# Streaming encoder trunk, one core: the MLP up projection with four PSUM banks, sums of squared outputs on VectorE, a new memory order at the turn to the MLP, and the last product gated from PSUM

## The chip, the cores and the metric

The kernel runs on one core of one Trainium2 chip. The metric is the device time of one execution in microseconds (us); smaller is better. Before the change the median of 3 runs is 2645.79 us (2639.45 to 2650.24). The profile is of one more execution, of 2640.47 us.

## The reference, cut to what matters

One layer: a modulated RMSNorm, an input projection shared by an mLSTM and a short convolution, an output projection, and then the squared-ReLU MLP that the change is about. 2048 prompt tokens and 128 sample tokens go through the same weights; sample tokens have their own modulation values (`mod`), one set for each group of 16 tokens.

```python
x = x + gt1 * (mix @ w_out)
h2 = _rms(x) * g2 * (1 + sc2) + sh2
x = x + gt2 * (jnp.square(jax.nn.relu(h2 @ w_up)) @ w_down)
...
y_prompt = _rms(xp) * g_final
```

D_MODEL is 1024, the MLP is 4096 wide, everything is float32.

## The kernel before, in words

**Attention.** The first stage (lines 200 to 830) does everything up to the first residual, in six blocks of tokens. It writes the residual x to DRAM (`x1s`) and a scale for each token (`x1r`). The up projection of the MLP begins when it has ended.

**Fast matrix product.** Each product of the MLP is made on 2x2 blocks with seven products in place of eight (a Winograd form), numbered 1 to 7, in the order of `ORDER` (L876): 1, 6, 5, 7, 2, 4, 3. A float32 operand is split in two float32r parts: ScalarE makes `hi` (L872, L1009, L1077), VectorE makes `lo = x - hi` (L873, L1010, L1078; GpSimd for two of the seven token operands, L1010), and TensorE does hi*hi, hi*lo and lo*hi (`mm12`, L934, every matmul is on L938).

**Up projection.** The tokens go in three passes p = 0, 1, 2 of two halves of 364, 364 and 360 tokens (`HALVES`). `stage_load` (L955) fetches the tokens of a pass, `stage_mod` (L969) multiplies by the scale (L972, on GpSimd) and applies the modulation (L979 to L982), `stage_split` (L984) makes the sums of blocks (L992, L993, L998, L1003) and the seven operands `h1` to `h7`. In each pass 16 units j = 0 to 15 follow (`up_unit`, L1013). A unit does the seven products, 12 matmuls each, so 84 matmuls. Its weights are fetched one unit ahead (`fetch_w`, L883) and split one unit ahead (`prep_w`, L896); in pass 0 the sums of weight blocks are also made (L902, four a unit) and written out (L903), and passes 1 and 2 read them back. In passes 1 and 2 sixteen calls of `sums_down` (L916) make the sums of the down weights: six in pass 1, ten in the first units of pass 2.

A unit has three PSUM banks, each with two buffers. Products 1 and 2 accumulate in bank 0, products 6, 7 and 4 in bank 1, products 5 and 3 in bank 2 (`where`, L1017). Between them VectorE reads the partial sums: product 7 adds onto 6 in the bank after L1028 has read it, product 4 adds onto 7 after L1030 has read it. Then ScalarE does ReLU and Square (L1039, L1040), GpSimd makes the sums of the squared outputs that the down projection needs (L1041 to L1043, three instructions), and SP's queue stores the tile (L1044).

**Down projection.** `open_down` (L1048) frees the memory of the up stage. Three passes of four groups g and seven products q follow; each of these 84 steps fetches a token operand (L1066) and a weight block (L1068), splits them (`d_prep`), does 2 x 24 matmuls (`d_mul`, L1082) and adds the result to an accumulator (L1095). In the last group, `combine` (L1107) joins accumulators and `close` (L1127) gates the result into y and adds its squares for the last RMSNorm (ScalarE L1146, GpSimd L1147). `final` (L1149) sums the squares over partitions on TensorE (L1153), scales y (L1159) and stores it (L1160).

**What sets the order.** TensorE runs in the order of the program. On the other engines the framework orders the instructions at build time by their place in the program and by when its own model of time has their inputs ready; each engine and SP's queue then run strictly in that order. Memory pools are laid out one behind the other; the MLP's pools lie over those of attention, and a tile waits for the tiles that it lies over to be dead (`open_up`, L940).

Of the kernel before, what the change touches and what calls it, by code (L numbers as in the profile page):

```python
# [9 lines left out]
F32 = mybir.dt.float32  # L10
# [34 lines left out]
def tile_hybrid(ctx: ExitStack, tc: tile.TileContext, xT, cst, early, rows_in, vgb, wada,  # L45
# [786 lines left out]
    def stats_last():  # L832
# [3 lines left out]
        ps = ps_.tile([128, 512], F32, name="st", tag="st")[:, :n]  # L836
# [39 lines left out]
    ORDER = (1, 6, 5, 7, 2, 4, 3)  # L876
# [63 lines left out]
    def open_up():  # L940
        pA.close()
        up = B["up"] = ctx.enter_context(ExitStack())

        def p(name, **kw):
            return up.enter_context(tc.tile_pool(name=name, reuse_waits="tile", **kw))

        B["ct"] = p("bct", bufs=2)
        B["nb"] = p("bnb", bufs=1)
        B["h"] = p("bh", bufs=1)
        B["stg"] = p("bstg", bufs=1)  # L950
        B["wr"] = p("bwr", bufs=1)
        B["wl"] = p("bwl", bufs=1)
        B["ps"] = p("bps", bufs=1, space=PSUM)

# [14 lines left out]
    def stage_mod(p, c, kh):  # L969
        t0, n = HALVES[2 * p + c]  # L970
        x = B["st"][:, c + 2 * kh, :, :n]
        pool.tensor_tensor(x, x, B["r"][:, c, :n].unsqueeze(1).to_broadcast([128, 4, n]), MUL)  # L972
        for k in range(4):
            kk = 4 * kh + k
            for a, b, smp in segments(t0, n):
                z = x[:, k, a:b]
                if smp:
                    z3 = z.rearrange("p (b s) -> p b s", b=NB)
                    dve.tensor_tensor(z3, z3, modT[:, 4, kk, 1:9].unsqueeze(2).to_broadcast([128, NB, TS]), MUL)  # L979
                    dve.tensor_tensor(z3, z3, modT[:, 3, kk, 1:9].unsqueeze(2).to_broadcast([128, NB, TS]), ADD)  # L980
                else:
                    act.activation(z, z, AF.Identity, scale=modT[:, 4, kk, 0:1], bias=modT[:, 3, kk, 0:1])  # L982

    def stage_split(p, q):  # L984
        n = HALVES[2 * p][1]
        st = B["st"]
        b11, b12, b21, b22, t2 = (st[:, j, :, :n] for j in range(5))
        i = ORDER[q]
        if i == 1:
            src = b11  # L990
        elif i == 6:
            dve.tensor_tensor(b12, b12, b11, SUB)  # L992
            dve.tensor_tensor(t2, b22, b12, SUB)  # L993
            src = t2
        elif i == 5:
            src = b12
        elif i == 7:
            dve.tensor_tensor(b11, t2, b11, SUB)  # L998
            src = b11
        elif i == 2:  # L1000
            src = b21
        elif i == 4:
            dve.tensor_tensor(b21, b21, t2, SUB)  # L1003
            src = b21
        else:
            src = b22
        hi = B["h"].tile([128, 4, HN], F32R, name=f"h{i}hi", tag=f"h{i}hi")[:, :, :n]
        lo = B["h"].tile([128, 4, HN], F32R, name=f"h{i}lo", tag=f"h{i}lo")[:, :, :n]
        act.activation(hi, src, AF.Copy)  # L1009
        (pool if q in (2, 5) else dve).tensor_tensor(lo, src, hi.bitcast(F32), SUB)  # L1010
        B["hc", i] = (hi, lo)

    def up_unit(p, j, between):  # L1013
        n = HALVES[2 * p][1]
        ct = B["ct"].tile([128, 7, n], F32, name="ct", tag="ct")
        banks = [B["ps"].tile([128, 512], F32, name=f"bk{z}", tag=f"bk{z}", bufs=2)[:, :n] for z in range(3)]
        where = {1: 0, 2: 0, 6: 1, 7: 1, 4: 1, 5: 2, 3: 2}  # L1017
        begun = {1, 6, 5}
        c11, c12, c21, c22 = (ct[:, z] for z in (0, 1, 2, 3))
        for q, i in enumerate(ORDER):  # L1020
            w, h = W[p, j, i], B["hc", i]
            bk = banks[where[i]]
            mm12(bk, [(w[0][:, k], w[1][:, k]) for k in range(4)], [(h[0][:, k], h[1][:, k]) for k in range(4)],
                 i in begun)
            if i == 1:
                act.activation(c21, bk, AF.Copy)
            elif i == 6:
                dve.tensor_tensor(c12, c21, bk, ADD)  # L1028
            elif i == 7:
                dve.tensor_tensor(c22, c21, bk, ADD)  # L1030
                dve.tensor_tensor(c22, c22, banks[2], ADD)
            elif i == 2:
                act.activation(c11, bk, AF.Relu)
            elif i == 4:
                dve.tensor_tensor(c21, c21, bk, ADD)
            elif i == 3:
                dve.tensor_tensor(c12, c12, bk, ADD)
# [44 lines left out]
    def d_mul(p, g, q, cd):  # L1082
# [24 lines left out]
    def combine(p, cd, i):  # L1107
# [12 lines left out]
        elif i == 4:  # L1120
            dve.tensor_tensor(a[4], a[7], a[4], SUB)  # L1121
            close(p, cd, 0, 1, a[4])
# [4 lines left out]
    def close(p, cd, ch, mh, z):  # L1127
        t0, n = HALVES[2 * p + ch]
        for c2 in range(2):
            k = 4 * mh + 2 * cd + c2  # L1130
            y = B["yt"][:, ch, k]
            for b0, b1, smp in segments(t0, n):
                d, yy = z[:, c2, b0:b1], y[:, b0:b1]
                if smp:
                    d3 = d.rearrange("p (b s) -> p b s", b=NB)
                    dve.tensor_tensor(d3, d3, modT[:, 5, k, 1:9].unsqueeze(2).to_broadcast([128, NB, TS]), MUL)
                    dve.tensor_tensor(yy, yy, d, ADD)
                else:
                    dve.scalar_tensor_tensor(yy, d, modT[:, 5, k, 0:1], yy, MUL, ADD)  # L1139
            if (p, ch) not in B["ssk"]:  # L1140
                B["ssk"].add((p, ch))
                B["ss", ch] = B["nb"].tile([128, HN], F32, name=f"ss{ch}", tag=f"ss{ch}")[:, :n]
                act.activation(B["ss", ch], y, AF.Square)
            else:
                sq = B["nb"].tile([128, HN], F32, name="bsq", tag="bsq", bufs=2)[:, :n]
                act.activation(sq, y, AF.Square)  # L1146
                pool.tensor_tensor(B["ss", ch], B["ss", ch], sq, ADD)  # L1147

    def final(p, ch):  # L1149
# [3 lines left out]
        pe.matmul(ps, ones, B["ss", ch], start=True, stop=True)  # L1153
# [220 lines left out]
```

## Time and profile before

| what | value |
|---|---|
| median of 3 runs | 2645.79 us |
| the profiled execution | 2640.47 us, span 2638.7 us |
| TensorE (PE) busy | 2424.5 us, 92% |
| VectorE (DVE) busy | 1930.8 us, 73% |
| ScalarE (ACT) busy | 1271.6 us, 48% |
| GpSimd (POOL) busy | 723.5 us, 27% |
| granted TensorE clock, mean | 0.969 |
| DMA | 540.75 MB, 205 GB/s |

The span is from the first to the last instruction. PE is the matrix engine, PEld its weight loads, SPq the queue of the engine that issues DMAs. A row of a group of instructions names line, engine, operation and tiles as out<-in; behind "|" come busy time and mean length, and the idle time of the engine just before. A row of a stretch gives its bounds and length, the busy time of PE, PEld, DVE, ACT and POOL with the number of their instructions, the mean granted TensorE clock as a share of full speed, the busy share of the DMA engines and what they moved. A row of a tile gives the shortest, median and longest instruction in ns.

### The profile page before, as it was taken

How to read it: one execution, taken by the hardware profiler on the slowest of the kernel's cores; microseconds unless marked ns; L12 is line 12 of the kernel's file. 1: busy time of each engine (PE TensorE's matmuls, PEld its weight loads, DVE VectorE, ACT ScalarE, POOL GpSimd, SP SyncE). 2: the span in 40 equal slices, each digit the busy share in tenths (PEclk: the TensorE clock that was granted, in tenths of full speed). 3: DMA queues.
4: the chain of work that ended last, by engine and by line, in shares of the span. 5: the costliest groups of instructions: out<-in, count | busy, mean ns of one | idle time of the engine just before them, and what ended most of it. 6: DMA issues, size and time to landing. Idle time of an engine off the chain costs nothing. (4 is left out here: it accounts for less than half of the span.)

```text
span 2638.7 us, 38838 instructions
## 1 busy us (share of the span) xinstructions
PE 2424.5 (92%) x14849; PEld 2349.5 (89%) x14849; DVE 1930.8 (73%) x2595; ACT 1271.6 (48%) x1989; POOL 723.5 (27%) x570
## 2 busy tenths in 40 slices
PE   7999899999999999579989989888899989999996
PEld 5899888999999999578889989888899989999996
DVE  5578876776767757787777677766647796788779
ACT  3455554544544535544455455434554455445443
POOL 1244433343423413442233243322300040002003
PEclk9999999999999999799999999999999999999998
DMA  7645466354353443456667875878776658657762
GB/s 298 207 136 195 137 215 212 109 175 127 90 191 107 135 134 111 148 198 223 233 209 245 311 247 202 285 255 298 261 267 228 227 176 313 228 192 272 263 234 101
DMA packets 208918, 540.75 MB, mean 205 GB/s; under 512 B 31632, under 2 KB 88464, under 8 KB 190300
## 3 DMA queue, kind: packets, MB, share of 16 engines
q1 hardware_dynamic: 203564, 514.33, 57.7%
q0 software_dynamic: 5168, 23.94, 2.7%
q8 instruction: 117, 1.92, 0.3%
q14 instruction: 69, 0.57, 0.1%
HBM read 420.83 MB, written 117.37 MB: 204 GB/s over the span
## 5 line engine op out<-in xcount | busy, mean ns | idle before, releaser
L872 ACT ACTIVATE whi<-wraw 128x512 fp32r<-128x512 f32 (+1 forms) x504 | 382.2, 771 | 593.4 <-PE dn L938 275.5
L873 DVE TENSOR_TENSOR wlo<-wraw,whi 128x512 fp32r<-128x512 f32 (+1 forms) x504 | 535.6, 1078 | 99.0 <-ACT whi L872 97.1
L938 PE MATMUL dn<-ulo,whi 128*128 128x364 f32 (+1 forms) x1344 | 445.0, 331 | 21.5 <-DVE ulo L1078 21.5
L938 PE MATMUL dn<-uhi,whi 128*128 128x364 f32 (+1 forms) x1344 | 446.3, 332 | 7.5 <-ACT uhi L1077 7.5
L938 PE MATMUL dn<-uhi,wlo 128*128 128x364 f32 (+1 forms) x1344 | 442.1, 329 | 0.0
L121 PE MATMUL mm<-hhi,whi 128*128 128x384 f32 (+1 forms) x1152 | 388.9, 338 | 1.1 <-DVE kT L462 0.7
L122 PE MATMUL mm<-hlo,whi 128*128 128x384 f32 (+1 forms) x1152 | 381.4, 331 | 0.0
L123 PE MATMUL mm<-hhi,wlo 128*128 128x384 f32 (+1 forms) x1152 | 380.1, 330 | 0.1
L80 ACT ACTIVATE whi<-wraw 128x1024 fp32r<-128x1024 f32 (+1 forms) x216 | 227.0, 1054 | 235.9 <-PE mm L122 142.5
L81 DVE TENSOR_TENSOR wlo<-wraw,whi 128x1024 fp32r<-128x1024 f32 (+1 forms) x184 | 243.9, 1328 | 93.3 <-ACT whi L80 92.9
L938 PEld LDWEIGHTS dn<-ulo,whi 128*128 128x128 f32 x1344 | 255.3, 190 | 24.5 <-DVE ulo L1078 24.3
L938 PEld LDWEIGHTS dn<-uhi,whi 128*128 128x128 f32 x1344 | 254.7, 189 | 8.2 <-ACT uhi L1077 7.8
L938 PEld LDWEIGHTS dn<-uhi,wlo 128*128 128x128 f32 x1344 | 255.6, 190 | 0.0
L1147 POOL TENSOR_TENSOR ss<-ss,bsq 128x364 f32<-128x364 f32 (+1 forms) x42 | 72.5, 1727 | 639.2 <-ACT bsq L1146 637.7
L121 PEld LDWEIGHTS mm<-hhi,whi 128*128 128x128 f32 x1152 | 219.4, 190 | 10.0 <-issue 6.8
L122 PEld LDWEIGHTS mm<-hlo,whi 128*128 128x128 f32 x1152 | 219.3, 190 | 0.7
L123 PEld LDWEIGHTS mm<-hhi,wlo 128*128 128x128 f32 x1152 | 219.1, 190 | 0.3 <-DVE wlo L81 0.3
L1041 POOL TENSOR_TENSOR ct<-ct 128x364 f32<-128x364 f32 (+1 forms) x48 | 49.3, 1027 | 496.6 <-ACT ct L1040 484.4
L1095 DVE TENSOR_TENSOR a<-a,dn 128x728 f32<-128x728 f32 (+1 forms) x126 | 114.4, 908 | 91.1 <-PE dn L938 87.6
L1078 DVE TENSOR_TENSOR ulo<-ur,uhi 128x1456 fp32r<-128x1456 f32 (+1 forms) x84 | 144.3, 1717 | 25.4 <-ACT uhi L1077 21.4
L122 PE MATMUL mm<-mlo,whi 128*128 128x384 f32 (+1 forms) x384 | 126.6, 330 | 3.9 <-POOL mlo L627 3.9
L123 PE MATMUL mm<-mhi,wlo 128*128 128x384 f32 (+1 forms) x384 | 127.1, 331 | 1.4 <-DVE wlo L81 1.3
(330 smaller groups left out, 5575.7 us busy)
## 6 DMA issues: line engine op xcount, KB each, us to landing
wraw<-wsd SPq DMA_DIRECT2D x48, 1024.0 KB, 4.9
wraw<-wup SPq DMA_DIRECT2D x160, 256.0 KB, 5.6
us<-ct SPq DMA_DIRECT2D x32, 1274.0 KB, 5.3
ur<-us SPq DMA_DIRECT2D x56, 728.0 KB, 5.6
wraw<-wbcx SPq DMA_DIRECT2D x72, 512.0 KB, 3.8
wraw<-wdown SPq DMA_DIRECT2D x36, 1024.0 KB, 5.0
wraw<-wsu SPq DMA_DIRECT2D x128, 256.0 KB, 5.9
wraw<-wout SPq DMA_DIRECT2D x48, 512.0 KB, 3.6
```

Source lines behind the costliest of these rows:

```text
L80: act.activation(hi[:, :n], raw[:, :n], AF.Copy)
L81: ins = eng.tensor_tensor(lo[:, :n], raw[:, :n], hi[:, :n].bitcast(F32), SUB).ins
L121: pe.matmul(out, lh[0], rh[0], start=first, stop=False)
L122: pe.matmul(out, lh[0], rh[1], start=False, stop=False)
L123: pe.matmul(out, lh[1], rh[0], start=False, stop=last)
L872: act.activation(hi, src, AF.Copy)
L873: dve.tensor_tensor(lo, src, hi.bitcast(F32), SUB)
L938: pe.matmul(out, lh, rh, start=first and z == 0, stop=z == len(seq) - 1, skip_group_check=not first)
L1041: pool.tensor_tensor(c12, c12, c11, SUB)
L1078: dve.tensor_tensor(lo, raw, hi.bitcast(F32), SUB)
L1095: dve.tensor_tensor(a, a, ps, ADD)
L1147: pool.tensor_tensor(B["ss", ch], B["ss", ch], sq, ADD)
```

## The change

- **Up banks.** Four banks of two buffers (two sets of four) in place of three. `ORDER` becomes 1, 6, 5, 7, 2, 3, 4. Products 1 and 2 share bank 0, 6 and 3 bank 1, 7 and 4 bank 3, 5 has bank 2. Product 3 starts its bank anew; only 2 and 4 add onto what the bank holds.
- **Sums of squared outputs.** Four VectorE instructions in place of three of GpSimd, made in the next unit after its second product, with the store behind them. One difference changes sign, and so does the use of product 4 in the down projection.
- **Tokens of a pass.** Three of the four scalings of `stage_mod` move from GpSimd to VectorE; the sample modulation is one instruction over four blocks in place of four; the sums of blocks become `stage_sum`, called at listed places; pass 1's tokens are loaded at unit 8 in place of 11; GpSimd makes the `lo` of products 3 and 4 in place of 5 and 4.
- **Memory.** The raw weight tiles come first in memory, the operands of products 1 and 6 last, and the other operands in a listed order.
- **Down projection, last group.** Before product 4, accumulator 7 is added to accumulator 4 and the sum is gated into y; product 4's own last group is then gated straight from PSUM. In the last pass, the last two squares are summed by TensorE; `final` of half 1 is called between the two halves of the last product.

```diff
-        ps = ps_.tile([128, 512], F32, name="st", tag="st")[:, :n]
+        ps = ps_.tile([128, 512], F32, name="st", tag="bk0", bufs=2)[:, :n]
...
-    ORDER = (1, 6, 5, 7, 2, 4, 3)
+    ORDER = (1, 6, 5, 7, 2, 3, 4)
...
+        B["wr"] = p("bwr", bufs=1)
         B["ct"] = p("bct", bufs=2)
         B["nb"] = p("bnb", bufs=1)
-        B["h"] = p("bh", bufs=1)
+        late, soon = p("bh", bufs=1), None
         B["stg"] = p("bstg", bufs=1)
-        B["wr"] = p("bwr", bufs=1)
         B["wl"] = p("bwl", bufs=1)
+        soon = p("bh16", bufs=1)
+        B["h"] = {i: soon if i in (1, 6) else late for i in ORDER}
...
-        pool.tensor_tensor(x, x, B["r"][:, c, :n].unsqueeze(1).to_broadcast([128, 4, n]), MUL)
+        eng = pool if (c, kh) == (0, 1) else dve
+        eng.tensor_tensor(x, x, B["r"][:, c, :n].unsqueeze(1).to_broadcast([128, 4, n]), MUL)
...
+    def stage_sum(p, z):
+        n = HALVES[2 * p][1]
+        b11, b12, b21, b22, t2 = (B["st"][:, j, :, :n] for j in range(5))
+        o, x, y = ((b12, b12, b11), (t2, b22, b12), (b11, t2, b11), (b21, b21, t2))[z]
+        dve.tensor_tensor(o, x, y, SUB)
...
-        (pool if q in (2, 5) else dve).tensor_tensor(lo, src, hi.bitcast(F32), SUB)
+        (pool if q > 4 else dve).tensor_tensor(lo, src, hi.bitcast(F32), SUB)
...
-        banks = [B["ps"].tile([128, 512], F32, name=f"bk{z}", tag=f"bk{z}", bufs=2)[:, :n] for z in range(3)]
-        where = {1: 0, 2: 0, 6: 1, 7: 1, 4: 1, 5: 2, 3: 2}
-        begun = {1, 6, 5}
+        banks = [B["ps"].tile([128, 512], F32, name=f"bk{z}", tag=f"bk{z}", bufs=2)[:, :n] for z in range(4)]
...
-            bk = banks[where[i]]
+            bk = banks[{1: 0, 2: 0, 6: 1, 3: 1, 5: 2, 7: 3, 4: 3}[i]]
             mm12(bk, [(w[0][:, k], w[1][:, k]) for k in range(4)], [(h[0][:, k], h[1][:, k]) for k in range(4)],
-                 i in begun)
+                 i not in (2, 4))
...
+            else:
+                o, x = {6: (c21, c21), 5: (c12, c21), 7: (c22, c12), 3: (c12, c12), 4: (c21, c21)}[i]
+                dve.tensor_tensor(o, x, bk, ADD)
             between(q)
         act.activation(ct[:, 1:4], ct[:, 1:4], AF.Relu)
         act.activation(ct[:, 0:4], ct[:, 0:4], AF.Square)
-        pool.tensor_tensor(c12, c12, c11, SUB)
-        pool.tensor_tensor(ct[:, 4], c22, c12, SUB)
-        pool.tensor_tensor(ct[:, 5:7], ct[:, 4:5].to_broadcast([128, 2, n]), ct[:, 0:3:2], SUB)
-        nc.sync.dma_start(us[p][j // 4][:, j % 4], ct.rearrange("p a b -> p (a b)"))
+
+        def sums():
+            dve.tensor_tensor(c12, c12, c11, SUB)
+            dve.tensor_tensor(ct[:, 4], c22, c12, SUB)
+            dve.tensor_tensor(ct[:, 5], ct[:, 4], c11, SUB)
+            dve.tensor_tensor(ct[:, 6], c21, ct[:, 4], SUB)
+            nc.sync.dma_start(us[p][j // 4][:, j % 4], ct.rearrange("p a b -> p (a b)"))
+
+        B["sums"] = sums
...
+            if mid and c2 == 0:
+                mid()
+        if g == 3 and i == 4:
+            with tc.high_priority():
+                close(p, cd, 0, 1, ps, True)
+            return
...
-        elif i == 4:
-            dve.tensor_tensor(a[4], a[7], a[4], SUB)
-            close(p, cd, 0, 1, a[4])
...
+            if late and cd and p == NP - 1:
+                B["more"].append(sq)
+            else:
                 pool.tensor_tensor(B["ss", ch], B["ss", ch], sq, ADD)
...
+        parts = [B["ss", ch], *(B["more"] if p == NP - 1 and ch == 0 else [])]
+        for z, sq in enumerate(parts):
+            pe.matmul(ps, ones, sq, start=z == 0, stop=z == len(parts) - 1)
+        v, y0, t, r = (nb.tile([128, HN], F32, name=f"f{z}", tag=f"f{z}", bufs=2)[:, :n] for z in "vytr")
...
+        hl = ("2hi", "2lo", "7hi", "3hi", "3lo", "4hi", "4lo", "7lo", "5lo", "5hi")
+        for z in hl:
+            late.tile([128, 4, HN], F32R, name=f"h{z}", tag=f"h{z}")
...
+            mods = ((10, 3), (11, 3), (12, 3), (13, 3)) if p == 0 else ((13, 1), (13, 4), (14, 1), (14, 3))
+            for at_, (c, kh) in zip(mods, parts):
+                z[at_] = [(stage_mod, (p + 1, c, kh))]
+            for at_, k in zip(((14, 0), (14, 2)) if p == 0 else ((14, 5), (14, 6)), (0, 1)):
+                z.setdefault(at_, []).append((stage_sum, (p + 1, k)))
+            for q in range(7):
+                z[15, q] = [(stage_sum, (p + 1, {3: 2, 6: 3}[q]))] if q in (3, 6) else []
+                z[15, q].append((stage_split, (p + 1, q)))
...
-            if j == 11 and p + 1 < NP:
+            if p + 1 < NP and j == (8, 11)[p]:
...
+                if q == 1 and before:
+                    before()
...
+            if g == 3 and ORDER[q] == 4:
+                for cd in range(2):
+                    a = B["a", p, 4, cd]
+                    dve.tensor_tensor(a, a, B["a", p, 7, cd], ADD)
+                    gate(p, cd, 0, 1, a)
...
-            d_mul(p, g, q, 1)
+            d_mul(p, g, q, 1, (lambda: final(p, 1)) if end else None)
...
         final(NP - 1, 0)
-        final(NP - 1, 1)
```

`gate` is the first half of the old `close`; it no longer writes the product of a sample segment in place, but into a tile `gs`.

## Rows read from the trace of the kernel before

**Rows 1.** Stretches: bounds, length, busy time by engine, clock, DMA share, GB/s.

```profile
1084.00:1108.00 24.00, 0.00 (x1) 0.00 (x0) 18.51 (x33) 10.66 (x23) 6.09 (x5) 0.55 0.53 169
1108.00:1134.00 26.00, 18.83 (x87) 17.58 (x88) 25.65 (x24) 14.00 (x18) 7.86 (x2) 0.82 0.22 70
1134.00:1367.00 233.00, 204.99 (x1177) 200.80 (x1176) 178.81 (x227) 112.74 (x170) 73.91 (x46) 0.96 0.64 224
1367.00:1409.00 42.00, 32.89 (x169) 32.29 (x168) 37.44 (x35) 23.75 (x29) 16.68 (x8) 0.84 0.50 166
1409.00:1625.00 216.00, 201.81 (x1179) 199.68 (x1178) 148.66 (x190) 113.37 (x170) 71.95 (x46) 0.98 0.79 273
...
1666.00:1833.00 167.00, 148.14 (x843) 143.37 (x841) 107.49 (x150) 70.57 (x104) 41.96 (x30) 0.96 0.82 287
1833.00:1908.00 75.00, 70.30 (x420) 68.49 (x419) 49.36 (x65) 40.74 (x59) 21.79 (x15) 1.00 0.74 258
1908.00:2613.00 705.00, 676.79 (x4017) 673.31 (x4018) 542.71 (x522) 338.45 (x346) 67.05 (x38) 0.98 0.67 233
2613.00:2638.70 25.70, 6.41 (x29) 4.47 (x27) 21.44 (x32) 5.93 (x12) 9.02 (x8) 0.69 0.29 115
...
1597.00:1625.00 28.00, 28.00 (x170) 28.00 (x169) 18.20 (x24) 14.93 (x22) 8.10 (x6) 1.00 0.65 223
```

**Rows 2.** What TensorE waited for, 1080 to 1910 us (total, times, longest).

```profile
PE bk L938 <- DVE ct L1030: 46.7, 20, 7.9
PE bk L938 <- DVE ct L1028: 33.1, 11, 5.0
PE bk L938 <- ACT h1hi L1009: 24.3, 1, 24.3
```

**Rows 3.** VectorE, then GpSimd, in order of time, 1139 to 1152 us (start, length).

```profile
1140.15 10.12 DVE L902 TENSOR_TENSOR wraw<-wraw 128x512 f32<-128x512 f32 x4
...
1151.40 0.52 DVE L1030 TENSOR_TENSOR ct<-ct,bk 128x364 f32<-128x364 f32 x1
...
1139.66 2.09 POOL L1043 TENSOR_TENSOR ct<-ct 128x728 f32<-128x728 f32 x1
1141.70 7.42 POOL L972 TENSOR_TENSOR stg<-stg,rst 128x1456 f32<-128x1456 f32 x2
```

**Rows 4.** Instructions of single tiles in the up stage (ns, min/median/max).

```profile
L873 DVE TENSOR_TENSOR wlo<-wraw,whi x332: 674/691/3800, 1123.7 to 1899.4; 128x512 fp32r<-128x512 f32 x164, 128x1024 fp32r<-128x1024 f32 x2
...
L1030 DVE TENSOR_TENSOR ct<-ct,bk x48: 515/520/533, 1129.1 to 1901.3; 128x364 f32<-128x364 f32 x32, 128x360 f32<-128x360 f32 x16
...
L1010 DVE TENSOR_TENSOR h7lo<-stg,h7hi x3: 1658/1660/1675, 1120.1 to 1645.4; 128x1456 fp32r<-128x1456 f32 x2, 128x1440 fp32r<-128x1440 f32 x1
```

**Rows 5.** Costliest VectorE groups, 1108 to 1910 us (busy, mean ns).

```profile
L873 DVE TENSOR_TENSOR wlo<-wraw,whi 128x512 fp32r<-128x512 f32 (+1 forms) x332 | 326.1, 1003 | 48.0 <-ACT whi L872 47.9
L902 DVE TENSOR_TENSOR wraw<-wraw 128x512 f32<-128x512 f32 x60 | 53.8, 907 | 7.4 <-DMA wraw<-wup 6.7
```

**Rows 6.** ScalarE in order of time at the turn to the MLP.

```profile
1106.30 0.63 ACT L872 ACTIVATE whi<-wraw 128x512 fp32r<-128x512 f32 x1 [6.88 <-DMA wraw<-wup]
1106.84 1.40 ACT L1009 ACTIVATE h1hi<-stg 128x1456 fp32r<-128x1456 f32 x1
```

**Rows 7.** The stretch with the fullest DMA engines, columns as in rows 1.

```profile
1500.00:1520.00 20.00, 17.85 (x108) 17.55 (x107) 11.08 (x18) 10.90 (x17) 4.47 (x4) 1.00 0.99 357
```

**Rows 8.** The chain that ended last, from the up to the down projection (start, length).

```profile
1903.88 9.26 DMA ur<-us
...
1916.39 13.67 PE dn L938 x72
```

**Rows 9.** The same chain behind the last matmuls.

```profile
2623.93 5.37 DVE y L1159 x8
...
2632.09 3.02 DVE y L1159 x6
```

**Rows 10.** ScalarE in order of time, a unit that began at 1245.0 us.

```profile
1247.56 1.40 ACT L1040 ACTIVATE ct<-ct 128x1456 f32<-128x1456 f32 x1
```

More of the change, by code (lines that the diff above doesn't have):

```diff
@@ new lines, in stage_mod @@
+        eng.tensor_tensor(x, x, B["r"][:, c, :n].unsqueeze(1).to_broadcast([128, 4, n]), MUL)
+        for a, b, smp in segments(t0, n):
+            if smp:
+                for v, op in ((4, MUL), (3, ADD)):
+                    z4 = x[:, :, a:b].rearrange("p k (b s) -> p k b s", b=NB)
+                    m4 = modT[:, v, 4 * kh:4 * kh + 4, 1:9].unsqueeze(3).to_broadcast([128, 4, NB, TS])
+                    dve.tensor_tensor(z4, z4, m4, op)
+            else:
+                for k in range(4):
+                    kk = 4 * kh + k
+                    act.activation(x[:, k, a:b], x[:, k, a:b], AF.Identity, scale=modT[:, 4, kk, 0:1],
+                                   bias=modT[:, 3, kk, 0:1])
@@ L1125, in combine, with gate @@
             close(p, cd, 1, 0, a[3])
-    def close(p, cd, ch, mh, z):
+    def gate(p, cd, ch, mh, z):
         t0, n = HALVES[2 * p + ch]
@@ L1134, in close @@
                 if smp:
-                    d3 = d.rearrange("p (b s) -> p b s", b=NB)
-                    dve.tensor_tensor(d3, d3, modT[:, 5, k, 1:9].unsqueeze(2).to_broadcast([128, NB, TS]), MUL)
-                    dve.tensor_tensor(yy, yy, d, ADD)
+                    t = B["nb"].tile([128, 128], F32, name="gs", tag="gs")
+                    t3 = t.rearrange("p (b s) -> p b s", b=NB)
+                    dve.tensor_tensor(t3, d.rearrange("p (b s) -> p b s", b=NB),
+                                      modT[:, 5, k, 1:9].unsqueeze(2).to_broadcast([128, NB, TS]), MUL)
+                    dve.tensor_tensor(yy, yy, t, ADD)
                 else:
                     dve.scalar_tensor_tensor(yy, d, modT[:, 5, k, 0:1], yy, MUL, ADD)
+    def close(p, cd, ch, mh, z, late=False):
+        n = HALVES[2 * p + ch][1]
+        gate(p, cd, ch, mh, z)
+        for c2 in range(2):
+            y = B["yt"][:, ch, 4 * mh + 2 * cd + c2]
             if (p, ch) not in B["ssk"]:
@@ L1143, in close @@
                 act.activation(B["ss", ch], y, AF.Square)
[L1144 to L1146 removed]
+                continue
+            sq = B["nb"].tile([128, HN], F32, name="bsq", tag="bsq", bufs=2)[:, :n]
+            act.activation(sq, y, AF.Square)
+            if late and cd and p == NP - 1:
+                B["more"].append(sq)
+            else:
                 pool.tensor_tensor(B["ss", ch], B["ss", ch], sq, ADD)
@@ L1183, in phase_b, with between @@
                 sums += 1
-            def between(q, p=p, j=j, nxt=nxt):
+            def between(q, p=p, j=j, nxt=nxt, before=B["sums"]):
                 if nxt:
                     prep_w(*nxt, q)
-                if p + 1 < NP:
-                    if j in (13, 14) and q in (1, 4):
-                        stage_mod(p + 1, *((0, 0), (1, 0), (1, 1), (0, 1))[2 * (j - 13) + (q == 4)])
-                    if j == 15:
-                        stage_split(p + 1, q)
+                if q == 1 and before:
+                    before()
+                for fn, args in plan.get(p, {}).get((j, q), ()):
+                    fn(*args)
                 if z == 0 and q == 2:
@@ L1196, in phase_b @@
             up_unit(p, j, between)
+        B["sums"]()
         assert sums == 16
@@ L1199, in phase_b @@
         B["ssk"] = set()
+        B["more"] = []
         ds = [(p, g, q) for p in range(NP) for g in range(4) for q in range(7)]
@@ L1204, in phase_b @@
         for z, (p, g, q) in enumerate(ds):
+            end = z + 1 == len(ds)
             if z + 2 < len(ds):
@@ L1208, in phase_b @@
                 y_load(p)
+            if g == 3 and ORDER[q] == 4:
[3 more added lines that the diff above has]
+                    gate(p, cd, 0, 1, a)
             d_mul(p, g, q, 0)
-            if z + 1 < len(ds):
+            if not end:
                 d_prep(*ds[z + 1])
```

63 lines of the change are left out of this document (17 added, 46 removed).

## The prediction

> **What bounds the kernel now.** I read the stretches first, then TensorE's waits, then single instructions of the engines that it waits for. Two full units of the up projection at an unbroken pace take 28.0 us [rows 1], so a unit costs 14.0 us when nothing holds TensorE, and 360/364 of that, 13.85 us, in pass 2. Against this the stretches show what is lost. The turn from attention and the first unit take 24 + 26 us for 14 us of work: 36 lost. Units 1 to 14 of pass 0 take 233 us for 196: 37 lost. The last unit of pass 0 with the first of pass 1 takes 42 us for 28, and the other change of pass, of 41 us, looks the same: 27 lost in both. Units 1 to 14 of pass 1 lose 216 - 196 = 20, the first ten after that in pass 2 167 - 138.5 = 28.5, the last five 75 - 69 = 6. That is 154 us in a stage where TensorE has nothing to wait for but other engines; the down projection with 705 us for some 4000 matmuls is close to its pace [rows 1]. The waits say for whom: 46.7 us for L1030 and 33.1 us for L1028, the reads of a bank that the next product adds onto, and 24.3 us for the first operand h1hi [rows 2]. The rest of the loss is the slow clock behind such a wait: 0.82 in the first unit, 0.84 at the change of pass, 0.96 in pass 0, of 2.4 GHz [rows 1].
>
> Why is L1030 late? It takes 0.52 us each time, but it stands in VectorE's queue behind L902 and L873, and these are held up: four L902 took 10.12 us in a row while GpSimd ran L1043 and two L972 of 7.42 us together [rows 3]. Alone, L873 takes 0.69 us, at most 3.80 [rows 4]; its mean is 1.00 us, so 332 of them lost about 104 us in the stage [rows 5]. L1030, which reads one input from PSUM, never took over 0.533 us [rows 4]. So an operation of VectorE with both inputs in SBUF waits for GpSimd's, and a PSUM read waits only in the queue.
>
> **The change, part by part.**
>
> Four banks. Product 7 no longer adds onto 6, and product 4 adds onto 7 with two products between them in place of one. The wait of 33.1 us has no more cause, and L1030's successor has 4.1 us in place of 2.1 us before it is missed. The number of reads stays at five a unit, of 0.52 us. The two sets fill all eight banks; unit j+1 writes the set that unit j-1 has left. The single reading of the sum for the last block's statistics takes one buffer of bank 0 once, hidden in unit 0's lost time.
>
> Sums on VectorE. Four instructions of 364 columns from SBUF; the nearest rows are 0.52 us for the same width with one input in PSUM and 0.69 us for 512 columns [rows 4]. I take 0.55, so 2.2 us a unit. VectorE then has in a unit of pass 0: seven L873 and four L902 of 0.69, five reads of 0.52, the sums: 7.6 + 2.6 + 2.2 = 12.4 us of 14.0. In pass 1 it is 9.7, with four more of 0.69 us in units that also sum down weights. This holds if GpSimd is quiet, and what is left to GpSimd is one L972 of 3.7 us a pass and two `lo`. The sums wait for ScalarE's Square; behind them in VectorE's queue stand the reads of products 6, 5 and 7. The Square of a unit ends 4.0 us into the next one [rows 10], just when the sums come up, so they should not wait. Their store follows in SP's queue, 2 us earlier than now.
>
> Units 1 to 14 of pass 0: of the 37 us I leave 4, for the three scalings (1.66 us each, as L1010 of the same width [rows 4]) and late weights: -33, between -5 (VectorE as now) and -37. Units 1 to 14 of pass 1: -15 of 20, between -4 and -20, since weights come by DMA here. First ten units of pass 2: they move 167 us x 287 GB/s = 47.9 MB [rows 1]; at the fullest stretch, 357 GB/s with DMA engines 0.99 busy [rows 7], that takes 134 us, hardly under the 138.5 us of TensorE. Between no gain and -28.5 I take half, -14. Last five units: -3 of 6.
>
> Changes of pass: in the last unit VectorE has 9.7 us of its own, five `lo` and two sums of blocks of 1.66 us [rows 4], in all 21 us against 14, and GpSimd still runs two `lo` that hold VectorE up. Some 7 us over is then lost each time in place of 13.5: -13, between 0 and -20.
>
> Turn from attention. The last matmul of attention ends at 1084; ScalarE made h1hi only at 1106.84, right behind a split that had waited 6.88 us for a weight of unit 1 [rows 6]. In the new memory order the operands of products 1 and 6 lie over attention tiles that are dead before its last product, and the weights' raw tiles over those of attention, of which the first are read by then. So h1 can be made before TensorE is free. Product 6 still needs all four scalings, and VectorE has in the first unit five `lo` and four sums of blocks (15 us), weight splits and sums of the next unit (7.6 us) and five reads (2.6 us): 25 us for 14. I leave 3 + 10 = 13 of the 36 us: -23, between -8 and -33.
>
> Start of the down projection. The first token operand was asked for at 1903.88, landed 9.26 us later, and TensorE began at 1916.4 [rows 8]. By my count of the pools its tile will lie over an operand of product 4, which is now the last to be read, at the end of the up stage, some 3.5 us later: +3.5, between 0 and +8.
>
> Last group of the down projection. For each half of product 4 an accumulation and a difference of 0.9 us go, an addition of 0.9 us and two more gates come; VectorE's work is the same within 1 us, and it is VectorE that ends the kernel: eight L1159 took 5.37 us, and the last six of the other half 3.02 us [rows 9]. `final` of half 1 can fill waits of the chain of half 0 in place of following it, but its matmul now stands inside the last product and may hold TensorE for 1 to 2 us until GpSimd's last sum. I take -3, between +2 and -8.
>
> Sum: -33 - 15 - 14 - 3 - 13 - 23 + 3.5 - 3 = -100.5, against the profiled execution's 2640.5 us: 2540 us. That execution lies 5.3 us under the median of the runs before, so a median may lie as much above my figure.
>
> **Rivals.**
>
> VectorE becomes the bound. It is busy for 178.8 of 233 us in pass 0, 37.4 of 42 us at the change of pass and 25.7 of 26 us in the first unit [rows 1], and it is given 48 x 2.2 = 106 us of GpSimd's work. If its operations stay as long as their means now, 1.00 and 0.91 us [rows 5], and the sums stretch alike to 0.75 us, a unit of pass 0 needs 7.0 + 3.6 + 2.6 + 3.0 = 16.3 us. Then pass 0 gains 37 - 14 x 2.3 = 5 us, the six units of pass 1 with down weights lose 14 so that 6 are gained, pass 2 gains 4, the changes of pass nothing: 2640.5 - 23 - 5 - 6 - 4 - 3 + 3.5 - 3 = 2600. For it speaks the busy share; against it rows 3, where the stretch goes with GpSimd's work, which leaves. The Trainium skill (Perfetto Trace Analysis, Optimizing Scalar/DVE Operations) advises the other direction, to offload a saturated VectorE to ScalarE or even GpSimd, which would make this the likelier case and 2600 the sum. The same paragraph warns that GpSimd and VectorE share an SBUF read port, so that moving work between the two might not help, and with that the trace agrees: 10.12 us of L902 beside 7.42 us of L972 [rows 3]. Chance 0.12.
>
> The memory order does not do what it says at the turn: h1hi still stands behind a split that waits for a weight, or the raw tiles over attention's bring the weights late. The 36 us stay, and the rest goes as forecast: 2563. For it, ScalarE ran h1hi in queue order behind a DMA [rows 6]. Chance 0.08.
>
> Slower: a ring through VectorE's queue. The sums stand ahead of the reads of products 6, 5 and 7; if Square comes late, VectorE stands still, product 4 waits for its bank, TensorE frees weight buffers late, ScalarE's splits wait for these and Square behind them comes late again. Product 4 begins 12 us into a unit, so with 2 us of sums this decides from a Square later than 10 us into the unit, against 4.0 us now [rows 10]. A stall of 2.1 us in each of 48 units takes back the 100.5 us; one of 3 us gives 2540 + 144 = 2684. Chance 0.04.
>
> **How the numbers follow.** The forecast has 0.76. Its own range, with the ends of the three largest terms not all at once, is 2512 to 2578. The range 2508 to 2600 adds the unshortened turn and half of the VectorE case; left out are the slower case, the other half and some of the forecast's own edges, together under 0.2. A measurement of this kernel tells some 0.5%, 13 us, from no change: faster than 2632 by the first three cases, 0.94; the slower case splits into 0.04 beyond and little near zero, to which I add 0.02 for small mishaps in sum.
>
> **What would show it.** Right: TensorE's waits for reads of banks fall from 80 us to under 20; L873's mean falls to about 0.72 us; units of pass 0 take 14.0 us; TensorE waits under 8 us at the turn; the ten units of pass 2 show DMA engines over 0.9 busy. The forecast is wrong if VectorE is over 95% busy in pass 0 with waits for wlo in place of the reads, if h1hi is again made over 15 us after attention's last matmul, or if VectorE waits for Square in most units.

## The result, and the profile after

The changed kernel takes 2567.4 us (median of four runs, 2566.9 to 2572.1), the kernel before 2647.7 in the same comparison: ratio 0.971, 95% interval 0.968 to 0.973. Its profiled execution took 2567.2 us with a span of 2565.1, so 73.6 us of span are gone (80.3 by the medians) where 100.5 were forecast. By stretch, as in [rows 1]:

```profile
1084.00:1092.00 8.00, 0.00 (x0) 0.00 (x0) 8.00 (x8) 4.67 (x12) 3.18 (x4) 0.75 0.60 179
1092.00:1122.00 30.00, 20.22 (x84) 18.00 (x85) 28.75 (x29) 15.32 (x20) 8.98 (x3) 0.73 0.43 144
1122.00:1325.00 203.00, 198.55 (x1182) 198.19 (x1181) 166.92 (x292) 112.69 (x174) 3.60 (x1) 0.99 0.72 253
1325.00:1363.00 38.00, 30.27 (x169) 29.41 (x168) 33.61 (x40) 23.29 (x30) 11.93 (x2) 0.93 0.68 227
1363.00:1560.00 197.00, 197.00 (x1177) 196.53 (x1176) 147.28 (x254) 113.11 (x170) 4.39 (x1) 1.00 0.88 305
1560.00:1596.00 36.00, 29.71 (x169) 28.85 (x168) 32.67 (x38) 23.31 (x29) 11.27 (x2) 0.96 0.46 158
1596.00:1753.00 157.00, 144.78 (x842) 142.73 (x841) 110.24 (x197) 73.58 (x107) 0.00 (x0) 0.97 0.90 314
1753.00:1822.00 69.00, 69.00 (x423) 68.97 (x421) 42.34 (x77) 35.72 (x52) 0.00 (x0) 1.00 0.68 253
...
1840.40:2565.10 724.70, 678.43 (x4002) 673.48 (x4000) 559.10 (x557) 338.35 (x352) 60.97 (x40) 0.97 0.64 224
```

Units 2 to 14 of pass 0, units 1 to 14 of pass 1 and the last five of pass 2 now run at TensorE's pace, with at most 0.7 us over in one of them. Unit 1 of pass 0 (20.2 us for 14.0) does not, nor do these: the turn (8 + 30 us), the changes of pass (38, and 36 for the other) and the first ten units of pass 2 (157 for 138.5). The last line is the down projection from its second step to the end: 724.7 us, before 713.0. It got longer, which no term of the sum foresaw.

What TensorE waits for, 1080 to 1910 us, beside [rows 2]:

```profile
PE bk L938 <- DVE ct L1021: 22.5, 9, 4.6
PE bk L938 <- ACT ct L1016: 12.2, 7, 2.6
PE bk L938 <- ACT whi L872: 11.1, 2, 8.7
...
PE bk L938 <- DVE wlo L873: 3.3, 2, 2.5
```

The reads of banks (now all L1021) cost 22.5 us for 80, and stand in the first units and at the changes of pass alone. New is L1016, ScalarE's copy of product 1. VectorE's own largest wait and then its groups, as in [rows 5]:

```profile
DVE ct L1027 <- ACT ct L1024: 67.4, 37, 2.7
```

```profile
L873 DVE TENSOR_TENSOR wlo<-wraw,whi 128x512 fp32r<-128x512 f32 (+1 forms) x355 | 260.7, 752 | 62.2 <-ACT whi L872 61.0
...
L902 DVE TENSOR_TENSOR wraw<-wraw 128x512 f32<-128x512 f32 x60 | 42.6, 727 | 3.8 <-DMA wraw<-wup 3.8
...
L1030 DVE TENSOR_TENSOR ct<-ct 128x364 f32<-128x364 f32 (+1 forms) x48 | 28.4, 591 | 0.0
```

L873 fell from 1003 to 752 ns, L902 from 907 to 727, and the four sums on VectorE have means between 0.53 and 0.65 us (L1030 0.59). Its first sum waits for Square (L1024) in 37 of 48 units. TensorE's waits in the down projection, first in the kernel before, from 1908 us on, then in the changed kernel, from 1820 us on:

```profile
PE dn L938 <- DVE ulo L1078: 21.5, 8, 4.0
PE st L1153 <- POOL ss L1147: 8.1, 2, 6.7
```

```profile
PE dn L938 <- DVE ulo L1067: 31.1, 7, 9.7
...
PE st L1158 <- POOL ss L1150: 3.2, 1, 3.2
```

### The profile page after: what moved, and what is told of

Read it like the earlier page. It is cut to its first block, busy times and chain, and to the rows that moved or that the text cites. A ratio compares the mean times of both kernels' runs of the same rounds, so it can differ in the third digit from the quotient of the medians.

```text
span 2565.1 us, 38873 instructions
## 1 busy us (share of the span) xinstructions
PE 2412.4 (94%) x14853; PEld 2346.2 (91%) x14853; DVE 1907.3 (74%) x2790; ACT 1269.8 (50%) x1989; POOL 489.5 (19%) x415
## 4 chain that ended last, share of the span: by engine, by line
PE 62%; DVE 18%; DMA 6%; issue 5%; ACT 5%; POOL 4%; SPq 0%; DVEq 0%; POOLq 0%; ACTq 0%
PE dn L938 23%; PE bk L938 15%; PE mm L121 7%; PE mm L122 7%; PE mm L123 7%; DMA us<-ct 3%; DVE wlo L873 2%; DMA wraw<-wup 2%; DVE wlo L81 2%; DVE y L1133 1%; DVE yc L644 1%; DVE ct L1021 1%; PE ada L262 1%; ACT whi L872 1%; POOL mt L188 1%
## 5 line engine op out<-in xcount | busy, mean ns | idle before, releaser
L873 DVE TENSOR_TENSOR wlo<-wraw,whi 128x512 fp32r<-128x512 f32 (+1 forms) x504 | 442.6, 891 | 94.7 <-ACT whi L872 91.7
L1150 POOL TENSOR_TENSOR ss<-ss,bsq 128x364 f32<-128x364 f32 (+1 forms) x40 | 61.0, 1528 | 897.9 <-ACT bsq L1146 896.8
L1090 DVE TENSOR_TENSOR a<-a,dn 128x728 f32<-128x728 f32 (+1 forms) x120 | 109.0, 908 | 91.6 <-PE dn L938 88.0
L1021 DVE TENSOR_TENSOR ct<-ct,bk 128x364 f32<-128x364 f32 (+1 forms) x240 | 126.2, 526 | 52.4 <-PE bk L938 49.4
```

The lines of the kernel that those rows point to most:

```text
L873: dve.tensor_tensor(lo, src, hi.bitcast(F32), SUB)
L1021: dve.tensor_tensor(o, x, bk, ADD)
L1090: dve.tensor_tensor(a, a, ps, ADD)
```

## The experiments

All start from the changed kernel. Times are medians, ratios stand against the kernel before in the same comparison. The kernel before has medians from 2641.7 to 2647.7 us in these comparisons, so rows of this table that lie 2 to 4 us apart (runs 4, 6, 7, 8 and 10 against the changed kernel) are not told apart by their times; for these the traces decide.

| run | us | ratio (95%) |
|---|---|---|
| changed kernel | 2567.4 | 0.971 (0.968 to 0.973) |
| 1 sums on GpSimd | 2618.6 | 0.990 (0.988 to 0.992) |
| 2 three banks | 2578.2 | 0.974 (0.972 to 0.977) |
| 3 both undone | 2632.9 | 0.995 (0.993 to 0.997) |
| 4 three scale tiles | 2565.2 | 0.970 (0.968 to 0.972) |
| 5 PSUM gate in last pass only | 2558.3 | 0.967 (0.966 to 0.969) |
| 6 no priority | 2565.2 | 0.970 (0.968 to 0.972) |
| 7 own tile for product 1 | 2569.7 | 0.971 (0.969 to 0.973) |
| 8 last add first | 2565.4 | 0.970 (0.967 to 0.972) |
| 9 down sums spread | 2548.7 | 0.964 (0.961 to 0.967) |
| 10 first scalings on VectorE | 2563.9 | 0.969 (0.966 to 0.972) |
| 11 four edits | 2530.0 | 0.958 (0.956 to 0.959) |
| 12 low parts on VectorE too | 2522.1 | 0.955 (0.953 to 0.956) |

**Runs 1 to 3: which half of the gain is whose.** In run 1 `sums()` issues on `pool`, as four instructions in the next unit (the kernel before had three, at the unit's end):

```diff
-            dve.tensor_tensor(c12, c12, c11, SUB)
+            pool.tensor_tensor(c12, c12, c11, SUB)
...
```

In run 2 the up projection has the old order and three banks; run 3 is both.

```diff
+    UORDER = (1, 6, 5, 7, 2, 4, 3)
...
-            bk = banks[{1: 0, 2: 0, 6: 1, 3: 1, 5: 2, 7: 3, 4: 3}[i]]
+            bk = banks[{1: 0, 2: 0, 6: 1, 7: 1, 4: 1, 5: 2, 3: 2}[i]]
...
+                if i == 7:
+                    dve.tensor_tensor(c22, c22, banks[2], ADD)
```

> The changed kernel with its four sums of squared outputs back on GpSimd, as four instructions of 364 columns; the four banks stay. Theory (the quiet GpSimd is the larger half of the gain in passes 0 and 1): GpSimd's sums again hold up VectorE's operations with two SBUF inputs, the mean of L873 goes from 0.89 to about 1.0 us, reads of banks come late, and the time rises by 20 to 45 us, to about 2595. Rival (the banks are the larger half: with 4 us of slack behind each read a late VectorE does no harm): at most +10 us, units of pass 0 stay at 14.0 to 14.3 us though L873 is as long as in the kernel before.

> The changed kernel with three banks, the old order of the seven products in the up projection, product 7 onto the bank of 6 and product 4 onto that of 7; the sums stay on VectorE. Theory (quiet GpSimd is the larger half): a read of a bank comes within its 2 us of slack most of the time, at most +12 us, to 2567 to 2580. Rival (banks are the larger half): the waits for the reads before products 7 and 4 come back though GpSimd is quiet, +25 us or more, to over 2592.

> Both undone: three banks with the old order of products, and the sums on GpSimd; scalings, memory order and the down projection as in the changed kernel. If the two parts add, the time is the changed kernel's plus the costs of the two single undoings; if each alone already frees TensorE (either slack or speed is enough), both single ones are cheap and this one costs 40 to 55 us, the gain measured in units 1 to 14 of passes 0 and 1 (31 and 19 us) and part of pass 2.

Sums back on GpSimd cost 51 us, three banks 11 by the medians and 2.7 by the spans of the profiled executions (2567.8 against 2565.1; the two intervals overlap), both together 65, so the parts add. By the end of the last product into a bank the up projection ends at 1822.3 us (changed), 1875.3 (run 1), 1826.1 (run 2) and 1889.2 (run 3). So the move of the sums is worth 53 us with four banks and 63 with three; the banks are worth 4 with quiet GpSimd and 14 beside its sums. The 4 is a lower end: the profiled execution of run 2 was its fastest, and the other three took 8 to 12 us more. The first theory holds, and its price was set too low (20 to 45 us). Run 1, TensorE's waits, then two groups of VectorE and GpSimd, 1108 to 1910 us:

```profile
PE bk L938 <- DVE ct L1021: 34.8, 16, 5.0
PE bk L938 <- ACT ct L1016: 19.2, 7, 3.9
```

```profile
L873 DVE TENSOR_TENSOR wlo<-wraw,whi 128x512 fp32r<-128x512 f32 (+1 forms) x341 | 294.4, 881 | 63.4 <-ACT whi L872 63.0
...
L1030 POOL TENSOR_TENSOR ct<-ct 128x364 f32<-128x364 f32 (+1 forms) x48 | 66.7, 1389 | 0.0
```

A sum of 0.59 us takes 1.39 us there, and VectorE's L873 grows again, from 752 to 881 ns (the expectation's 0.89 is the mean over the whole changed kernel). Even with product 4 two products behind its bank's read, reads come too late: in units 1 to 14 of passes 0 and 1 they are TensorE's only wait, 13.2 and 10.1 us, against 4.4 and none in the changed kernel. The rest of run 1's price has other places: the 19.2 us for L1016 all stand in the first ten units of pass 2, and at each change of pass 4.9 us are a wait for GpSimd's own h4lo. Runs 2 and 3, the same wait with three banks:

```profile
PE bk L939 <- DVE ct L1022: 37.4, 24, 4.4
```

```profile
PE bk L939 <- DVE ct L1022: 82.6, 35, 5.9
```

82.6 us (run 3) is about what the kernel before had in [rows 2]; with GpSimd quiet (run 2) it is 37.4 in 24 waits, against 22.5 with four banks.

**Runs 4, 8 and 10: the turn.** The changed kernel makes h1hi at 1078.9, yet TensorE, whose last matmul of attention ends at 1083.3, stands until 1092. ScalarE, then VectorE, in order of time:

```profile
1090.96 0.52 ACT L162 ACTIVATE sq<-x 128x384 f32<-128x384 f32 x1 [2.77 <-DVE x L202]
1091.39 0.61 ACT L872 ACTIVATE whi<-wraw 128x512 fp32r<-128x512 f32 x1
...
1086.29 1.66 DVE L993 TENSOR_TENSOR stg<-stg 128x1456 f32<-128x1456 f32 x1
1087.87 2.46 DVE L1002 TENSOR_TENSOR h1lo<-stg,h1hi 128x1456 fp32r<-128x1456 f32 x1
1090.26 0.60 DVE L202 SCALAR_TENSOR_TENSOR x<-mm,modT,x 128x384 f32<-128x384 f32 x1
```

The first weight's split stands behind attention's last Square, and this behind the last addition in VectorE's queue. My first reading was another: the weight was fetched only at 1085, since SyncE's queue held loads of pass 1's scales (L969) that waited for their tile.

```diff
-        r = B["stg"].tile([128, 2, HN], F32, name="rst", tag="rst")
+        r = B["stg"].tile([128, 2, HN], F32, name="rst", tag="rst", bufs=3)
```

> The changed kernel with three tiles for the token scales (L969) in place of one. Theory (SyncE's queue is what makes the turn 8 us long): the loads of the scales for pass 1 no longer stand in SyncE's queue from 1068 to 1083 us ahead of the first weights, these are asked for by about 1070, land by 1076, and product 1 begins as soon as attention's last matmul is over and h1hi is made, so TensorE's 8.0 us without work go to 0 to 2. Of this 5 to 8 us reach the end: 2559 to 2563. Rival (VectorE, busy 28.75 of the 30 us of the first unit, ends that unit whenever product 1 begins): the wait goes, but the first unit gets longer by as much, 2565 to 2569.

Run 4, SyncE, then ScalarE:

```profile
1071.42 4.67 SPq L894 DMA_DIRECT2D wraw<-wup  x4
...
1091.42 0.61 ACT L872 ACTIVATE whi<-wraw 128x512 fp32r<-128x512 f32 x1
```

The fetch came 14 us earlier and the split did not: that theory falls. Run 8 puts the last addition ahead, with the edit of run 4:

```diff
+        with tc.issue_after(hcur["ga"]):
+            for z in (0, 1):
+                stage_sum(0, z)
```

(and the same around the first `stage_split`; `hcur["ga"]` is the last L202).

> The kernel with three tiles for the token scales, and in it attention's last gated addition (L202) put ahead of the first sums of blocks and of h1lo in VectorE's queue. Theory (what holds the first weight split is ScalarE's queue: attention's last Square, which waits for that addition, stands before it): the split runs at 1086 to 1088 us in place of 1091.4 and TensorE's wait at the turn falls from 8 us to 3 or 4; VectorE, which ends the first unit, starts on the same list of work some 2 us earlier or none, so of this 0 to 3 us reach the end: 2560 to 2566. Rival (nothing but this queue makes the first two units long): the first two units end 4 us or more earlier, and the time is under 2560.

In this execution attention's last matmul ended at 1085.6 us, 2.3 later than in the changed kernel and in run 4, so the times count from there. The split ran 5.2 us behind it in place of 8.1 (at 1090.8; the additions still stood behind a scaling, at 1087.5 and 1088.6), TensorE waited 5.9 us for it in place of 8.7, and the third unit began 58.7 us behind it, just as in run 4 (59.3 in the changed kernel). The wait got shorter and the units behind it longer by as much: the queue order alone is worth nothing, since VectorE is busy for 28.75 of the 30 us of the first unit. Run 10 starts VectorE's work earlier:

```diff
-        eng = pool if (c, kh) == (0, 1) else dve
+        eng = pool if p and (c, kh) == (0, 1) else dve
```

> The changed kernel with all four token scalings of pass 0 on VectorE; the one on GpSimd took 4.33 us, and ScalarE's modulations stood behind it. Theory (from 1078 to 1143 us VectorE is busy for 60 of 65 us and sets the end of the first two units; it stands idle before, and work that reaches it earlier ends earlier): h1hi is made some 2 to 4 us sooner, VectorE's list starts sooner by as much, and the third unit begins at 1139 to 1141 us in place of 1142.6; the time is 2563 to 2566. Rival (VectorE's extra 1.7 us eats what the earlier start gives): the third unit begins at 1142 to 1145, no change.

```profile
1069.33 1.43 ACT L1001 ACTIVATE h1hi<-stg 128x1456 fp32r<-128x1456 f32 x1
```

h1hi came 9.6 us sooner, and the third unit began at 1135.4: 7.2 us earlier, or 6.2 counted from attention's last matmul, which ended 1.0 us sooner in this execution. That is more than expected. The span fell by only 4.7 us, since the ten units of pass 2 took 2.7 more.

**Runs 7 and 9: pass 2.** ScalarE's waits in the changed kernel, 1596 to 1753 us:

```profile
ACT ct L1016 <- DMA us<-ct: 29.3, 8, 4.7
ACT whi L872 <- DMA wraw<-wsu: 23.8, 10, 3.6
```

The copy of product 1 waits for the store of the tile that it writes. Run 7 gives it a tile of its own:

```diff
-                act.activation(c21, bk, AF.Copy)
+                m1 = B["ct"].tile([128, HN], F32, name="m1", tag="m1")[:, :n]
+                act.activation(m1, bk, AF.Copy)
...
-                o, x = {6: (c21, c21), 5: ...
+                o, x = {6: (c21, m1), 5: ...
```

> The changed kernel with the copy of product 1 (ScalarE L1016) into a small tile of its own in place of a part of ct; the read of product 6 adds from there, so ScalarE need not wait until the store of ct of two units earlier has landed. Theory (in pass 2 TensorE waits for this copy, which waits for that store): the 12.2 us of waits for L1016 go, the ten units of pass 2 take 139 to 146 us in place of 157, and the time is 2553 to 2560. Rival (the DMA queue is the bound of these ten units, so the read of product 6 into ct, or a weight, waits instead): the ten units stay over 152 us and the time at 2563 to 2570.

The ten units took 157.2 us: the rival. The wait moved. Run 7, TensorE over the up projection and ScalarE in the ten units:

```profile
PE bk L938 <- DVE ct L1022: 33.2, 16, 4.6
...
ACT whi L872 <- DMA wraw<-wsu: 35.0, 11, 5.5
```

Run 9 leaves the waits and takes bytes away from these units:

```diff
-            if (p == 1 and j < 11 and j % 2 == 0) or (p == 2 and j < 15 and sums < 16):
+            if (p == 1 and j < 11 and j % 2 == 0) or (p == 2 and j < 15 and j % 3 < 2 and sums < 16):
```

> The changed kernel with the ten sums of down weights of pass 2 spread over its first fourteen units, two in every three, in place of one in each of the first ten. Theory (after the change the first ten units of pass 2 move more bytes than the DMA queues deliver at TensorE's pace, and the wait that showed it, ScalarE's copy behind a store, was only the place where the lack appears): with a third fewer of these bytes per unit the units return to 13.9 us, the fifteen units after the first of pass 2 take 208 to 214 us in place of 225.8, and the time is 2553 to 2559. Rival (it is not the rate: SyncE's queue holds the store back whenever a store of sums stands ahead of it): each unit with sums is as long as now, the fifteen units stay at 223 us or more and the time at 2563 to 2570.

The ten units, bounds and columns as in the first table:

```profile
1597.50:1735.60 138.10, 138.10 (x842) 138.10 (x842) 104.19 (x191) 73.97 (x110) 0.00 (x0) 1.00 0.92 328
```

All of the loss is gone, for the same sums within the same pass, and units with sums take 13.8 us like those without, so the rival falls. The gain is larger than expected (2548.7 us for 2553 to 2559). The changed kernel moves 157 us x 314 GB/s = 49.3 MB in ten units, which at TensorE's pace would take 357 GB/s; 328 it gets without a wait.

**Runs 5 and 6: the down projection.** The 9.7 us wait, VectorE in the changed kernel at the first change of pass:

```profile
2065.61 1.67 DVE L1240 TENSOR_TENSOR a<-a,a 128x728 f32<-128x728 f32 x1
...
2068.91 1.09 DVE L1133 SCALAR_TENSOR_TENSOR y<-dn,modT,y 128x364 f32<-128x364 f32 x2
2069.92 1.21 DVE L873 TENSOR_TENSOR wlo<-wraw,whi 128x1024 fp32r<-128x1024 f32 x1
2071.05 2.42 DVE L1067 TENSOR_TENSOR ulo<-ur,uhi 128x1456 fp32r<-128x1456 f32 x1
```

The gates of product 4 stand before the first operand of the next pass. Run 5 goes back to the accumulated way in all passes but the last; run 6 only drops the priority.

```diff
-        if g == 3 and i == 4:
+        if g == 3 and i == 4 and p == NP - 1:
...
-            with tc.high_priority():
-                close(p, cd, 0, 1, ps, True)
+            close(p, cd, 0, 1, ps, True)
```

(The first pair is run 5, which also gets its old closing and leaves out the gates ahead; the second is run 6.)

> The changed kernel, with product 4 of the down projection gated straight from PSUM in the last pass only; in the first two passes it is accumulated and closed as in the kernel before. Theory (the gates from PSUM and the gates ahead of them stand in VectorE's queue before the splits wlo and ulo of the next pass's first steps; this is where the down projection lost some 12 us): TensorE's waits for ulo of 9.7 and 8.1 us go back to under 4, the down projection to some 713 us from its second step to the end, the time to 2554 to 2558. Rival (the reversed order of products 3 and 4 or the sums of squares make the wait, wherever the gates read): no change, 2563 to 2570.

> The changed kernel without the raised priority around the closing of product 4 in the down projection; what is computed from PSUM stays. If the priority alone puts these gates ahead of the splits, the waits for ulo at the two changes of pass fall as without the gates from PSUM, 2554 to 2560, and the end of the kernel may lengthen by 1 to 3 us. If it is the work itself (four gates more for each pass, and three buffers of dn that must be read), the waits stay within 2 us and the time within 4.

From its second step to the end the down projection takes 717.3 us in run 5 and 722.1 in run 6, against 724.7 (723.5 to 725.6 in the profiles that leave it as it is). The work is the cause, with 7.4 us; the priority is worth 2.6 at most. Run 5, TensorE's waits from 1820 us on:

```profile
PE dn L938 <- DVE ulo L1067: 17.5, 6, 4.0
PE st L1161 <- POOL ss L1153: 9.2, 3, 4.2
```

No wait for ulo is longer than 4.0 us, as in the kernel before. But of the 9.2 us for the sums of squares of `final`, 5.9 stand at the two changes of pass (1.8 at 2075 us and 4.2 at 2314 us), where neither the kernel before nor the changed one waits for them; this takes back part of the gain.

**Runs 11 and 12.** Run 11 joins runs 5, 9 and 10, and moves `final` of the first passes from steps 0, 1 to steps 2, 3. Run 12 adds one line:

```diff
-        (pool if q > 4 else dve).tensor_tensor(lo, src, hi.bitcast(F32), SUB)
+        dve.tensor_tensor(lo, src, hi.bitcast(F32), SUB)
```

> Four edits of the changed kernel together: gates from PSUM in the last pass only, the sums of down weights spread over fourteen units, all scalings of pass 0 on VectorE, and the first two finals one pair of steps later in the down projection, so that TensorE's sum does not wait for GpSimd's last addition there (9.2 us in three waits when the gates of the first passes were taken back). If the gains add, 2567.4 - 18 (spread) - 7 (gates) - 5 (scalings) - 0 to 5 (finals) = 2532 to 2538. Rival (what is saved early is waited for again at the next stage): over 2545.

> The same with the low parts of the operands of products 3 and 4 (h3lo, h4lo, L1002) on VectorE in place of GpSimd, in all three passes. Theory (at a change of pass VectorE is late because GpSimd holds it: an operation of 0.52 to 0.68 us took 3.4 us beside h3lo and beside h4lo): 2 x 1.66 us are added to VectorE and some 2 x 2.8 us of holding go, and product 3 no longer waits for GpSimd; each change of pass and the first unit get 2 to 4 us shorter, 6 to 10 us less than the four edits alone. Rival (VectorE has 21 us of work for 14 at a change of pass, and more work is only more): no change or up to 5 us more.

The gains add: 18.7, 9.1 and 3.5 us alone by the medians, 37.4 together with the moved `final`, which is 2 us below the expected range. The down projection takes 714.6 us from its second step to the end, and no wait for `final` is left at the changes of pass. Run 12 takes off 7.9 more, and the reason shows in the changed kernel, GpSimd and VectorE at a change of pass:

```profile
1339.42 8.63 POOL L1002 TENSOR_TENSOR h3lo<-stg,h3hi 128x1456 fp32r<-128x1456 f32 x1 [202.59 <-ACT h3hi L1001]
1353.41 3.29 POOL L1002 TENSOR_TENSOR h4lo<-stg,h4hi 128x1456 fp32r<-128x1456 f32 x1 [5.36 <-ACT h4hi L1001]
...
1345.21 3.38 DVE L873 TENSOR_TENSOR wlo<-wraw,whi 128x512 fp32r<-128x512 f32 x1
...
1353.69 3.40 DVE L1028 TENSOR_TENSOR ct<-ct 128x364 f32<-128x364 f32 x1
```

Run 12, the two changes of pass, against 39.4 and 36.4 us in run 11:

```profile
1316.00:1351.00 35.00, 30.56 (x171) 29.68 (x170) 32.08 (x44) 23.63 (x29) 0.00 (x0) 0.94 0.66 229
...
1548.50:1582.50 34.00, 30.14 (x171) 29.26 (x170) 31.54 (x43) 23.65 (x29) 0.00 (x0) 0.95 0.51 173
```

## Why the prediction was right, and where it was not

The direction, the mechanism and the range hold; the sum was 27 us too large. Term by term, forecast and measured (from the starts of the units; the measured ones add up to the 73.6 us):

- Units 1 to 14 of pass 0: -33, and -31. Of pass 1: -15, and -19. Last five: -3, and -5.3. Right, and in units 1 to 14 by the cause named, VectorE's operations held by GpSimd: runs 1 and 3 show it. What the text did not weigh is how unequal the parts are: "The wait of 33.1 us has no more cause" credits the banks, and without them most of the waits for reads stay away too (run 2: 37.4 us in all, for 22.5 with the banks and 79.8 before).
- Turn from attention and first unit: -23, and -11.5, of which 0.7 are attention's, whose last matmul ended sooner. This is the second largest miss. The step "I leave 3 + 10 = 13 of the 36 us" counted 25 us of VectorE's work for a unit of 14 and then left only 10 us over for it, with 3 of wait; it was 8.7 of wait and 16 over. Work of the turn that stands before the unit, and what GpSimd's h3lo and h4lo do to VectorE, are missing in it. h1hi was made before TensorE was free, as forecast; it was not what TensorE then waited for. Runs 4 and 8 exclude both queues as what sets the end, runs 10 and 12 show VectorE's list.
- Changes of pass: -13, and -8.7. The step "GpSimd still runs two `lo` that hold VectorE up. Some 7 us over" was 9.3 us over each time (74.5 us for 56 in both); in run 12 these two `lo` alone are worth 4.5 and 2.4 us.
- First ten units of pass 2: -14, and -10. "Between no gain and -28.5 I take half" was a choice between bounds; that the rate is the bound holds (run 9). The wait that showed it was no part of the text.
- Start of the down projection: +3.5, and -0.3: from the last product of the up projection to the second step it takes 18.2 us, before 18.5. Nothing came of the later tile.
- Last group and the rest of the down projection: -3, and +11.7, the largest miss. The last step to the end took 34.7 us, before 35.1, so the 3 us hoped for there were 0.4. The step that failed is "VectorE's work is the same within 1 us": it was costed at the kernel's end, where nothing follows, and not at the two changes of pass, where the same gates stand before the next pass's ulo: the first three steps of passes 1 and 2 took 4.6 and 6.4 us longer than before.

Of the signs for the forecast, units of 14.0 us came up in pass 0 from unit 2 on, and L873 came near its mark (0.75 us for 0.72). Three came out at or just beyond their marks: the waits for reads at 22.5 us for under 20, the wait at the turn at 8.7 for under 8, the DMA engines in the ten units at 0.90 for over 0.9. One sign that the text named against itself came up: VectorE waits for Square in most units. "just when the sums come up, so they should not wait" was wrong, by 1.8 us in each of 37 units; but units of 14.0 us show that nobody missed the reads behind it, and no ring formed, as that rival's 10 us had put it.

The rival that VectorE becomes the bound is false for whole passes. In the first unit (busy for 28.75 of 30 us) and at the changes of pass (33.6 of 38 and 32.7 of 36) it is near the truth, but there a part of the busy time is GpSimd's holding: run 12 gives VectorE two operations more and these stretches get shorter. The Trainium skill (Perfetto Trace Analysis, Optimizing Scalar/DVE Operations) says that giving work of a saturated VectorE to ScalarE or even GpSimd may make sense, and warns that between VectorE and GpSimd it might not help. The runs decide for the warning and further: work taken from GpSimd and given to VectorE saved 51 us (run 1) and 8 us (run 12 against 11). The Trainium skill (SBUF — State Buffer, Who interferes with whom) names a reason: a VectorE instruction with two SBUF inputs contends with a GpSimd instruction that reads SBUF, because its second input comes through the read interface that the two share, and one with at most one SBUF input does not. The traces agree: L1028 took 3.40 us for 0.52 beside h4lo, while the reads of banks, with one input in SBUF, have a mean of 0.53 us and never took over 0.54 in any of these runs.

What stays open: of the 11.7 us in the down projection run 5 gives back 7.4. Moving `final` was only tried together with other edits: run 11 gives back 2.7 more, where runs 9 and 10 alone leave the down projection at 723.5 and 724.1 us; the last 1.7 us are not explained. And no run undoes the new memory order or the moved scalings, so how the gain at the turn divides between them is not shown.

## What to carry to other kernels

Before giving VectorE's work to GpSimd, look at what VectorE's operations with two SBUF inputs take beside it: four sums of 0.53 to 0.65 us were cheaper on VectorE, which is busy with them for 167 of 203 us in pass 0, than on GpSimd, which has 3.6 us of work there without them. A wait that the profile names may only be where a lack comes up: take the wait away and it moves (run 7), take the load away and it goes (run 9). And when a step is costed at one place, look for every other place where the same code runs, and for what stands behind it in the queue there.

## What was not expected of the hardware

GpSimd does not only hold VectorE, it is held by it: h3lo took 8.63 us while VectorE ran most of its list beside it at the usual lengths, h4lo 3.29 while VectorE's L1028 stood still. The DMA engines gave 328 GB/s over 138 us with TensorE never waiting, and 314 over 157 us when 357 were wanted, though single stretches of 20 us reached 357 [rows 7]. The Trainium skill (DMA: Bandwidth & Descriptors, Where 436 GB/s comes from) puts HBM's limit for a core at some 358 GB/s, half of what two cores share; estimated by that figure the 49.3 MB of the ten units just fit into 138 us, and measured they did not. For short stretches it is no ceiling here, where one core runs: slices of 3.5 us in run 9's ten units reach 440 GB/s.
